# RWKV chains: four buffers for keys and products, a later second product, and another layout of the stage's tiles

## The chip, the cores and the metric

The kernel runs on one core of a Trainium2 chip. The metric is the device time of one execution in microseconds (us); less is better. A core has five engines that run side by side, each through its own list of instructions in order: TensorE (PE, matmuls, with its weight loads shown as PEld), VectorE (DVE), ScalarE (ACT), GpSimd (POOL) and SyncE (SP). SP does nothing but issue DMA transfers, one after another; 16 DMA engines carry them out. Instructions wait for each other through semaphores.

## The reference

One inference step of a backbone with four layers (retention, RWKV-7 time mixing, differential attention, neighbourhood attention), each for 128 context tokens and 512 latent tokens, 640 in all, of width 1024. The change touches the second layer, RWKV-7, whose core is this scan, for 16 heads of width 64, forwards and backwards in time:

```
def step(s, inp):
    r_t, w_t, k_t, v_t, kk_t, a_t = inp
    sa = jnp.einsum('bhvk,bhk->bhv', s, -kk_t)
    s = (s * w_t[:, :, None, :] + sa[..., None] * (kk_t * a_t)[:, :, None, :]
         + v_t[..., None] * k_t[:, :, None, :])
    return s, jnp.einsum('bhvk,bhk->bhv', s, r_t)
```

The sum of both directions is normalised by head, a bonus term is added, and the result goes through a gate and the output projection.

## The kernel before, in words

The layer has two parts. The first, `rwkv_project`, computes the projections and, pair of heads by pair of heads (eight pairs), the scaled queries and keys; `rwkv_prepare` writes them to DRAM (`wd_q`, `wd_bk`, and the pieces `wd_lt`, `wd_lb` of a triangular matrix). The second part, `rwkv_mix`, reads them back and runs the chains. Time is cut into 10 chunks of 64 tokens; within a chunk the scan becomes small matrix products, with the inverse of a triangular 64 x 64 matrix for each chunk, direction and head, and only a short chain from chunk to chunk is left. The steps of a pair p in `rwkv_mix` are:

- `rwkv_inverse` (L1300): inverts the 32 x 32 diagonal blocks by 31 steps of two vector instructions, a product into `wtmp` (L1312) and a subtraction from `wX` (L1314). It loads `wN` (L1306), stores the inverse (L1315), copies its transpose into `wN` (ACT, L1317) and stores that (L1318). For pairs 0 to 2 DVE does it during the projections; for pairs 3 to 7 it is POOL, during the chains. There `wN` has two buffers and `wX` has one.
- `inverses` (L1380): loads the inverted blocks into `wTT` (L1390) and `wLB`, `wTM` (L1385, L1386), and makes the off-diagonal blocks by two sets of 80 small matmuls (L1398). The first set's result goes into `wPZ` (L1403), the second's, from `wPZ` and `wTT`, into `wTT` (L1405 on DVE, L1407 on ACT).
- `scores` (L1408): loads the keys `wKK` (L1414), the products `wBK` (L1415) and the queries `wR` (L1417); transposes the keys (L1424) into `wQT`, multiplies keys with BK (L1431, masked into `wQT`, L1433), `wQT` with `wTT` (L1441), BK with R (L1449), scales BK and transposes it into `wBT` (L1473); loads the values `wUV` and their copy `wRS` and the start states.
- `chain` (L1494): eight steps, each a set of matmuls (L1504), a copy on ACT, a set of matmuls (L1511) and updates on DVE.
- `read` (L1527) and `finish` (L1542): the outputs into the PSUM tile `wy`, the normalisation on DVE, two multiplications on POOL (with `wgb`, L1565, and with the bonus, L1567), a transposition (L1570), the gate `wsg` (L1572) and the store (L1573).

Tiles of one name share buffers: a new one waits until the last user of the buffer is done. `wKK` and `wBK` have two buffers, and each pair takes two, one for each direction. Most others have one for even and one for odd pairs. All of them lie in SBUF in the order of the list `order2`, with those that it doesn't name (`wN`, `wX`, `wtmp`, `wyc` and small ones) after them; ahead of the list come the mask, the first `wTT`, `wTM`, `wPZ` and two `wLB`, 20.75 KB for each partition. The first part of the layer used the same stretch of SBUF from the left, in the order `wxx` (20 KB), `wN`, `wX`, `wBK`, `wQ`, `wLT` and so on, with the projection weights and the hidden state from the right. The layer after it puts the output projection's weights (`wr`, `wh`, `wl`) at the right again.

The order of instructions on each engine, SP's among them, is fixed when the kernel is built: a planner simulates the run and takes, of what it holds to be ready, the instruction with the smallest priority number. `at` (L1578) sets that number: 2000 for each pair, and an offset for each step (`phase`: the chain -3, `inverses` -2.2, `scores` and the inverse -2, `finish` -1.3, `read` -0.4).

Of the kernel before, what the change touches and what calls it, by code (L numbers as in the profile page):

```python
# [10 lines left out]
AF = mybir.ActivationFunctionType  # L11
ALU = mybir.AluOpType
# [8 lines left out]
NT = 640  # L21
# [1021 lines left out]
NCH = 10  # L1043
# [29 lines left out]
class Rwkv:  # L1073
# [260 lines left out]
    def rwkv_mix(s, dr, od):  # L1334
        nc, I, O = s.nc, s.I, s.O
        v, act, pe, gp = nc.vector, nc.scalar, nc.tensor, nc.gpsimd
        H = (slice(0, 64), slice(64, 128))
        LO, HI = H
        with s.pool('w2') as w2, s.pool('w2p', space=PSUM) as pp:
            T = lambda shape, name, bufs=1, dt=F32: w2.tile(shape, dt, name=name, tag=name, bufs=bufs)  # L1340
            P = lambda name, bufs, shape=(128, 512): pp.tile(list(shape), F32, name=name, tag=name, bufs=bufs)
            z = lambda shape, name, dt=F32: w2.tile(shape, dt, name=name)
            inverse = lambda p: p in s.inv_late and s.rwkv_inverse(T, dr, p, 2)

            u64, u128 = [128, 2, 20, 64], [128, 2 * NCH, 128]
            bt, rr, qa = [128, NCH, 128], [128, 2, NCH, 2, 64], [128, 2 * NCH, 2, 64]
# [3 lines left out]
            TTs = [z(u128, 'wTT0')]  # L1350
            TM, PZ = z([128, 2 * NCH, 32], 'wTM'), z([128, 2 * NCH, 32], 'wPZ')
            LBs = [z([128, 2 * NCH, 32], f'wLB{k}') for k in range(2)]
# [3 lines left out]
            for k in s.order2:  # L1356
                if k == 'TT1':
                    TTs.append(z(u128, 'wTT1'))
                elif k == 'fin':
                    for n, sh, b in (('vt', [128, 5, 128], 1), ('sg', [128, NT], 1), ('yc', [128, 10, 64], 1), ('gb', [128, 128], 1), ('SW', [128, 4, 64], 2),  # L1360
                                     ('st0', [128, 64], 2), ('SF', [128, 2, 64], 1), ('so', [64, 2, 64], 2)):
                        T(sh, 'w' + n, b)
                elif k == 'misc':
                    for n, sh, b in (('gb', [128, 128], s.fin_bufs['gb']), ('st0', [128, 64], s.st_bufs), ('SF', [128, 2, 64], 1), ('so', [64, 2, 64], s.st_bufs)):
                        T(sh, 'w' + n, b)
                elif k[:3] == 'pad':
                    w2.tile([128, int(k[3:])], F32, name='w' + k)
                elif k in ('vt', 'sg'):
                    T([128, 5, 128] if k == 'vt' else [128, NT], 'w' + k, s.fin_bufs[k])
                elif k[0] == 'R' and k[1] in '01':  # L1370
                    Rs[int(k[1])][int(k[2])] = query(int(k[1]), int(k[2]))
                else:
                    T({'QT': u128, 'KK': [128, NCH, 64], 'BK': [128, NCH, 128], 'RR': rr, 'QA': qa, 'BT': bt, 'RS': u64, 'UV': u64}[k[:2]], 'w' + k,
                      2 if k in ('KK', 'BK') else 1)
            for t in (*TTs, *Rs[0], *Rs[1]):
                gp.memset(t, 0.0)
            st_ = {}
# [2 lines left out]
            def inverses(p):  # L1380

                TT, LB, tt_d, tq_d = TTs[p % len(TTs)], LBs[p % 2], dr['tt'][p], dr['tq'][p]
                for h in range(2):
                    a = h * 64
                    nc.sync.dma_start(out=LB[a:a + 32], in_=dr['lb'][p][h])  # L1385
                    nc.sync.dma_start(out=TM[a:a + 32], in_=tq_d[h].rearrange("u s t -> s u t"))  # L1386
                for blk in (1, 0):
                    for h in range(2):
                        a = h * 64 + blk * 32
                        nc.sync.dma_start(out=TT[a:a + 32, :, a:a + 32], in_=tt_d[blk, h].rearrange("u s t -> s u t"))  # L1390

                for prod in range(2):
                    ps = [P('wtp', 2, (128, 16, 32)) for _ in range(2)]
                    for u in range(20):
                        for h in range(2):
                            a = slice(h * 64 + 32 * prod, h * 64 + 32 * prod + 32)
                            l, r = (LB[a, u, :], TM[a, u, :]) if prod == 0 else (PZ[a, u, :], TT[a, u, h * 64 + 32:h * 64 + 64])
                            pe.matmul(ps[h][u % 4 * 32:u % 4 * 32 + 32, u // 4, :], l, r, start=True, stop=True)  # L1398
                    for h in range(2):
                        for j in range(4):  # L1400
                            src = ps[h][j * 32:j * 32 + 32, :5, :]
                            if prod == 0:
                                (v.tensor_copy if h else act.copy)(PZ[h * 64 + 32:h * 64 + 64, j::4, :], src)  # L1403
                            elif h:
                                v.tensor_scalar(out=TT[64:96, j::4, 96:128], in0=src, scalar1=-1.0, scalar2=None, op0=ALU.mult)  # L1405
                            else:
                                act.activation(out=TT[0:32, j::4, 32:64], in_=src, func=AF.Copy, scale=-1.0)  # L1407
            def scores(p):  # L1408
                cols = slice(p * 128, p * 128 + 128)
                KK, BK, R, BT = {}, {}, Rs[p % 2], {}  # L1410
                QT, RR = T([128, 2 * NCH, 128], 'wQT'), T(rr, f'wRR{p % 2}')
                for d in range(2):
                    KK[d], BK[d] = T([128, NCH, 64], 'wKK', 2), T([128, NCH, 128], 'wBK', 2)
                    nc.sync.dma_start(out=KK[d].rearrange("p c t -> p (c t)"), in_=dr['q'][p][d, 0])  # L1414
                    nc.sync.dma_start(out=BK[d].rearrange("p c t -> p (c t)"), in_=dr['bk'][p][d])  # L1415
                    for i in range(2):
                        nc.sync.dma_start(out=R[d][H[i], :, i, :], in_=dr['q'][p][d, 1, H[i]].rearrange("p (c t) -> p c t", t=64))  # L1417

                QTp = QT.rearrange("p (q i) k -> p q (i k)", i=2)
                for q0 in range(0, NCH, 4):  # L1420
                    n = min(4, NCH - q0)
                    ps = P('wtp', 2, (128, 4, 128))
# [4 lines left out]
                for d in range(2):  # L1427
                    pa = [P('wsc', 2, (128, 8, 64)) for _ in range(2)]
                    for c in range(NCH):
                        for i in range(2):  # L1430
                            pe.matmul(pa[i][H[c % 2], c // 2, :], KK[d][H[i], c, :], BK[d][H[i], c, 64:128], start=True, stop=True)  # L1431
                    for i in range(2):
                        v.tensor_tensor(out=QTp[:, d * 5:d * 5 + 5, 64 + i * 64:128 + i * 64], in0=pa[i][:, :5],  # L1433
                                        in1=mask[:, 0:1, :].to_broadcast([128, 5, 64]), op=ALU.mult)

                TT = TTs[p % len(TTs)]
                QA = T(qa, f'wQA{p % 2}')
                for u0 in range(0, 20, 4):
                    ps = P('wsc', 2, (128, 4, 128))
# [4 lines left out]
                for d in range(2):  # L1444
                    for c0 in range(0, NCH, 4):
                        n = min(4, NCH - c0)
                        ps = P('wsc', 2, (128, 4, 128))
# [4 lines left out]
                for d in range(2):  # L1452
# [16 lines left out]
                    for c0 in range(0, NCH, 4):  # L1469
                        n = min(4, NCH - c0)  # L1470
                        ps = P('wtp', 2, (128, 4, 128))
# [4 lines left out]
                for i in range(2):  # L1476
                    for d in range(2):
                        src = dr['vr' if d else 'v'][:, cols].rearrange("(c t) (i d) -> i t c d", t=64, i=2)[i]
# [4 lines left out]
                for d in range(2):  # L1483
                    st = T([128, 64], 'wst0', s.st_bufs)
                    nc.sync.dma_start(out=st, in_=I['state_rwkv'][0, 0, d, 2 * p:2 * p + 2].rearrange("i v k -> (i v) k"))
                    ps = P('wtp', 2, (128, 8, 64))
# [91 lines left out]
            def at(part, fn, p, *args):  # L1578
                s.tc.cur_priority = first + int(s.scale * (p + s.phase[part]))
                return fn(p, *args)  # L1580

            at('inv', inverse, 0)
            at('whole', inverses, 0)
            at('score', scores, 0)
            at('inv', inverse, 1)
            at('whole', inverses, 1)
            at('score', scores, 1)
            at('inv', inverse, 2)
            for p in range(8):
                at('chain', chain, p)  # L1590
                if p < 6:
                    at('whole', inverses, p + 2)
                ps = at('read', read, p)
                if p < 6:
                    at('score', scores, p + 2)
                    if p < 5:
                        at('inv', inverse, p + 3)
                at('fin', finish, p, ps)
# [171 lines left out]
class Kernel(Net, Ret, Rwkv, Diff, Na, Run):  # L1770
    hp = (600, 1, 1, 1, 300, 0, 0)
    preps = {'r': (2, 2, 2, 2)}
    bkv = 1
    order2 = ('KK', 'BK', 'RR1', 'QT', 'QA1', 'BT00', 'UV0', 'BT10', 'RS0', 'BT01', 'BT11', 'R01', 'RS1', 'R10', 'UV1', 'R11', 'TT1', 'QA0', 'RR0', 'R00', 'misc', 'pad448', 'vt', 'sg')
    todo_ret = [(0, 4), (0, 5), (1, 0), (1, 1), (1, 2), (1, 3), (1, 4), (1, 5)]
    todo_rwkv = []
    todo_t = {0: [(2, 0), (2, 1), (2, 2), (2, 3), (2, 4), (2, 5)], 1: [(3, 0), (3, 1), (3, 2), (3, 3), (3, 4), (3, 5)]}
# [28 lines left out]
    scale = 2000  # L1806
# [37 lines left out]
```

## Time and profile before

| | |
|---|---|
| median of 3 runs | 2563.71 us (2556.4 to 2573.88) |
| the profiled execution's own time | 2563.22 us |
| its span, first to last instruction | 2561.5 us |
| PE busy | 2314.2 us (90%), 18951 matmuls |
| DVE, ACT, POOL busy | 1442.0 (56%), 1115.7 (44%), 730.3 us (29%) |
| mean granted clock of TensorE | 0.935 of full speed |
| DMA | 303.54 MB in 353575 packets, 150489 of them under 512 B |

Busy time is the time in which an engine had an instruction in work, and an engine that waits for another is not busy. The shares are means over four layers with different limits, so the stage of the change has to be read by itself.

### The profile page before, as it was taken

Reading aid. Unit: us, or ns where it says so; the run is one execution under the profiler, and the core shown is the slowest. Engines: PE = TensorE matmul, PEld = TensorE weight load, DVE = VectorE, ACT = ScalarE, POOL = GpSimd, SP = SyncE. Lnnn points to the kernel's source line nnn. Section 1 sums busy time; section 2 is a strip of 40 time slices with the busy share of each in tenths; the row PEclk is TensorE's granted clock in tenths of the full one; section 3 lists DMA queues with packets and bytes.
Section 4 is the critical chain, followed back from the end, with each engine's and each line's share of the span. In section 5 each row is a group of like instructions: output and inputs, shape, how many; then the busy total and the mean of one; then the engine's idle time right before and its main releaser. Section 6 shows DMA issues by size and latency. Waiting matters only on the chain. (4 is left out here: it accounts for less than half of the span.)

```text
span 2561.5 us, 48738 instructions
## 1 busy us (share of the span) xinstructions
PE 2314.2 (90%) x18951; PEld 2086.4 (81%) x18951; DVE 1442.0 (56%) x3369; ACT 1115.7 (44%) x2565; POOL 730.3 (29%) x694
## 2 busy tenths in 40 slices
PE   7999999997989899876988887899898898999998
PEld 4889898987959789776877777588888888898888
DVE  6534344443173888772555564667766665654454
ACT  5323333333144655544545442345555534655551
POOL 3323232413210000013666503333323233333221
PEclk9999999998999889987879988899999998999999
DMA  8432333325273467756454634511111122322221
GB/s 292 132 109 89 110 115 114 106 80 191 79 245 107 130 211 214 221 172 155 135 145 128 169 109 149 179 54 56 48 47 48 44 74 60 78 76 65 76 72 58
DMA packets 353575, 303.54 MB, mean 119 GB/s; under 512 B 150489, under 2 KB 291313, under 8 KB 353345
## 3 DMA queue, kind: packets, MB, share of 16 engines
q1 hardware_dynamic: 353344, 300.44, 39.6%
q8 instruction: 149, 2.44, 0.4%
q14 instruction: 82, 0.66, 0.1%
HBM read 231.37 MB, written 64.79 MB: 116 GB/s over the span
## 5 line engine op out<-in xcount | busy, mean ns | idle before, releaser
L93 POOL TENSOR_TENSOR wl<-wr,wh 128x1024 fp32r<-128x1024 f32 (+1 forms) x168 | 371.8, 2227 | 668.2 <-ACT wh L170 526.6
L88 PE MATMUL pj<-hH,wh 128*128 128x320 f32 x1280 | 405.8, 319 | 11.0 <-ACT hH L96 7.6
L89 PE MATMUL pj<-hL,wh 128*128 128x320 f32 x1280 | 405.2, 317 | 2.7 <-POOL hL L93 1.8
L90 PE MATMUL pj<-hH,wl 128*128 128x320 f32 x1280 | 402.3, 315 | 0.1
L88 PEld LDWEIGHTS pj<-hH,wh 128*128 128x128 f32 x1280 | 244.7, 192 | 24.6 <-ACT hH L96 10.8
L89 PEld LDWEIGHTS pj<-hL,wh 128*128 128x128 f32 x1280 | 245.0, 191 | 10.5 <-POOL hL L93 4.6
L90 PEld LDWEIGHTS pj<-hH,wl 128*128 128x128 f32 x1280 | 244.9, 191 | 2.3 <-issue 1.0
L170 ACT CAST wh<-wr 128x1024 fp32r<-128x1024 f32 x168 | 175.4, 1047 | 122.0 <-PE pj L89 52.7
L88 PE MATMUL oa<-oh,wh 128*128 128x384 f32 (+1 forms) x640 | 200.3, 314 | 18.8 <-ACT wh L170 14.7
L88 PE MATMUL pj<-wh,hH 128*128 128x256 f32 x640 | 190.4, 298 | 13.0 <-DVE dr L756 8.5
L89 PE MATMUL oa<-ol,wh 128*128 128x256 f32 (+1 forms) x640 | 198.1, 311 | 0.7 <-DVE ol L93 0.6
L90 PE MATMUL oa<-oh,wl 128*128 128x256 f32 (+1 forms) x640 | 197.7, 311 | 0.0
L89 PE MATMUL pj<-wl,hH 128*128 128x256 f32 x640 | 188.0, 294 | 0.0
L90 PE MATMUL pj<-wh,hL 128*128 128x256 f32 x640 | 187.5, 293 | 0.0
L88 PEld LDWEIGHTS pj<-wh,hH 128*128 128x128 f32 x640 | 129.8, 203 | 21.1 <-DVE dr L756 9.6
L88 PEld LDWEIGHTS oa<-oh,wh 128*128 128x128 f32 x640 | 121.8, 191 | 22.2 <-ACT wh L170 15.0
L89 PE MATMUL pj<-wxl,wh 128*128 128x320 f32 x416 | 132.9, 322 | 4.2 <-DVE wxl L93 4.2
L90 PE MATMUL pj<-wxh,wl 128*128 128x320 f32 x416 | 131.7, 320 | 1.2 <-DVE wl L93 1.2
L88 PE MATMUL pj<-wxh,wh 128*128 128x320 f32 x416 | 131.4, 324 | 1.0 <-ACT wxh L96 1.0
L89 PEld LDWEIGHTS pj<-wl,hH 128*128 128x128 f32 x640 | 129.7, 203 | 0.0
L90 PEld LDWEIGHTS pj<-wh,hL 128*128 128x128 f32 x640 | 129.6, 202 | 0.0
L89 PEld LDWEIGHTS oa<-ol,wh 128*128 128x128 f32 x640 | 122.1, 191 | 1.5 <-DVE ol L93 1.3
(480 smaller groups left out, 5633.0 us busy)
## 6 DMA issues: line engine op xcount, KB each, us to landing
wr<-in_ret_w_in SPq DMA_DIRECT2D x48, 512.0 KB
wm<-in_w_mod SPq DMA_DIRECT2D x40, 512.0 KB
wr<-in_w_mod SPq DMA_DIRECT2D x32, 512.0 KB
wr<-in_rwkv_w_in SPq DMA_DIRECT2D x32, 512.0 KB
wl<-in_w_mod SPq DMA_DIRECT2D x24, 512.0 KB
wr<-in_diff_w_in SPq DMA_DIRECT2D x48, 256.0 KB
wr<-in_na_w_in SPq DMA_DIRECT2D x48, 256.0 KB
wd_bk<-wBK SPq DMA_DIRECT2D x16, 640.0 KB
```

The lines of the kernel that those rows point to most:

```text
L88: mm(out, l[0], r[0], start=start, stop=False)
L89: mm(out, l[0], r[1], start=False, stop=False)
L90: mm(out, l[1], r[0], start=False, stop=stop)
L93: eng.tensor_tensor(out=lo, in0=src, in1=hi.bitcast(F32), op=ALU.subtract)
L170: nc.scalar.copy(hi[:, :, :n], raw[:, :, :n])
```

## The change

Five edits, all for `rwkv_mix`. `wKK` and `wBK` get four buffers each. The late inverses' `wN` gets one buffer (the default of `rwkv_inverse`) in place of two. The second set of small matmuls of the inverse, with its copies, becomes a function `product(p, 1)` that `scores` calls after the masked products and before the product of `wQT` with `wTT`; the first stays in `inverses`. The list `order2` is sorted anew: KK and BK go from its head almost to its end, the small tiles (`misc`: `wgb`, start and end states), `wvt` and `wsg` go from its end into its middle, `wyc` is named there too, and a pad of 1.75 KB goes. No instruction is added or removed.

```diff
-            inverse = lambda p: p in s.inv_late and s.rwkv_inverse(T, dr, p, 2)
+            inverse = lambda p: p in s.inv_late and s.rwkv_inverse(T, dr, p)
...
-                elif k in ('vt', 'sg'):
-                    T([128, 5, 128] if k == 'vt' else [128, NT], 'w' + k, s.fin_bufs[k])
+                elif k in ('vt', 'sg', 'yc'):
+                    T({'vt': [128, 5, 128], 'sg': [128, NT], 'yc': [128, 10, 64]}[k], 'w' + k, s.fin_bufs.get(k, 1))
...
-                      2 if k in ('KK', 'BK') else 1)
+                      4 if k in ('KK', 'BK') else 1)
...
-                for prod in range(2):
-                    ps = [P('wtp', 2, (128, 16, 32)) for _ in range(2)]
-                    for u in range(20):
...
+                product(p, 0)
+
+            def product(p, prod):
+
+                TT, LB = TTs[p % len(TTs)], LBs[p % 2]
+                ps = [P('wtp', 2, (128, 16, 32)) for _ in range(2)]
+                for u in range(20):
...
-                    KK[d], BK[d] = T([128, NCH, 64], 'wKK', 2), T([128, NCH, 128], 'wBK', 2)
+                    KK[d], BK[d] = T([128, NCH, 64], 'wKK', 4), T([128, NCH, 128], 'wBK', 4)
...
                         v.tensor_tensor(out=QTp[:, d * 5:d * 5 + 5, 64 + i * 64:128 + i * 64], in0=pa[i][:, :5],
                                         in1=mask[:, 0:1, :].to_broadcast([128, 5, 64]), op=ALU.mult)
+                product(p, 1)
...
-    order2 = ('KK', 'BK', 'RR1', 'QT', 'QA1', 'BT00', 'UV0', 'BT10', 'RS0', 'BT01', 'BT11', 'R01', 'RS1', 'R10', 'UV1', 'R11', 'TT1', 'QA0', 'RR0', 'R00', 'misc', 'pad448', 'vt', 'sg')
+    order2 = ('RR1', 'QT', 'QA1', 'BT00', 'UV0', 'BT10', 'RS0', 'misc', 'vt', 'sg', 'yc', 'BT01', 'BT11', 'R01', 'RS1', 'R10', 'UV1', 'R11', 'TT1', 'RR0', 'KK', 'BK', 'QA0', 'R00')
```

## Rows read from the trace of the kernel before

**Rows 1.** Stretches: length; busy PE, PEld, DVE, ACT, POOL; granted clock; DMA share; GB/s.
```profile
1144.00:1157.00 13.00, 0.71 (x22) 0.61 (x15) 2.63 (x11) 2.97 (x5) 2.24 (x1) 0.50 0.79 241
1157.00:1176.00 19.00, 16.95 (x188) 14.79 (x187) 5.38 (x10) 12.15 (x33) 1.26 (x1) 0.91 1.07 192
...
1192.00:1500.00 308.00, 282.48 (x4531) 240.95 (x4530) 175.46 (x498) 157.88 (x407) 186.32 (x342) 0.87 0.53 137
...
1386.00:1426.00 40.00, 35.54 (x623) 29.62 (x621) 21.38 (x60) 21.41 (x56) 28.88 (x56) 1.00 0.55 145
```

**Rows 2.** Waits of PE from 1135 to 1565: total us, times, longest.
```profile
PE wsc L1431 <- issue: 13.4, 1, 13.4
PE wy L1570 <- DVE wyc L1568: 12.5, 3, 12.0
PE wtp L1424 <- DMA wKK<-wd_q: 12.3, 1, 12.3
PE wsc L1431 <- DMA wBK<-wd_bk: 5.2, 4, 1.9
...
PE wtp L1398 <- DVE wPZ L1403: 2.3, 2, 1.7
...
PE wtp L1424 <- DVE wTT L1405: 2.1, 2, 1.2
PE wtp L1398 <- DMA wR<-wd_q: 1.8, 1, 1.8
```

**Rows 3.** Timeline of the entry: start, length, instruction, [idle before, what ended it].
```profile
1133.05 0.31 PE L90 MATMUL pj<-wxh,wl 128*128 128x320 f32 x1
...
1147.62 0.29 SPq L1318 DMA_DIRECT2D wd_tq<-wN  x1
...
1149.29 1.00 SPq L1415 DMA_DIRECT2D wBK<-wd_bk  x2
...
1156.54 1.30 PE L1424 MATMUL wtp<-ident,wKK 128*128 128x128 f32 x5 [12.29 <-DMA wKK<-wd_q]
...
1187.26 2.04 SPq L1306 DMA_DIRECT2D wN<-wd_lt  x2
1189.43 0.34 SPq L1415 DMA_DIRECT2D wBK<-wd_bk  x1
1189.82 1.08 PE L1431 MATMUL wsc<-wBK,wKK 64*64 64x64 f32 x26 [13.42 <-issue]
...
1192.96 0.23 POOL L1312 TENSOR_TENSOR wtmp<-wX,wN 80x31 f32<-80x31 f32 x1 [28.19 <-DMA wN<-wd_lt]
```

**Rows 4.** DMA from 1138 to 1192.
```profile
DMA packets 21127, 10.68 MB, mean 198 GB/s; under 512 B 18522, under 2 KB 19290, under 8 KB 21124
```

**Rows 5.** Waits of SP's queue from 1200 to 1480: total us, times, longest.
```profile
SPq L1415 <- PE wtp L1473: 31.7, 7, 12.9
```

**Rows 6.** Timeline, all engines, from one late inverse to the next.
```profile
1402.52 0.27 POOL L1314 TENSOR_TENSOR wX<-wX,wtmp 80x31 f32<-80x31 f32 x1
...
1404.83 0.29 SPq L1318 DMA_DIRECT2D wd_tq<-wN  x1
...
1406.82 0.23 POOL L1312 TENSOR_TENSOR wtmp<-wX,wN 80x31 f32<-80x31 f32 x1
...
1407.55 0.85 SPq L1386 DMA_DIRECT2D wTM<-wd_tq  x2
```

**Rows 7.** The tile wX, 1190 to 1460: min/median/max ns, first and last start.
```profile
L1314 POOL TENSOR_TENSOR wX<-wX,wtmp x155: 247/587/1125, 1193.3 to 1450.2; 80x31 f32<-80x31 f32 x10, 80x60 f32<-80x60 f32 x10, 80x87 f32<-80x87 f32 x10, 80x112 f32<-80x112 f32 x10
```

**Rows 8.** Timeline of PE: the first product of QT and TT of pair 7.
```profile
1477.69 1.62 PE L1441 MATMUL wsc<-wTT,wQT 128*128 128x128 f32 x12
```

**Rows 9.** The tile wTT, copies of the second product on DVE: min/median/max ns.
```profile
L1405 DVE TENSOR_SCALAR wTT<-wtp x32: 315/321/329, 1145.6 to 1474.0; 32x160 f32<-32x160 f32 x32
```

**Rows 10.** Timeline of ACT at the exit: casts of the output projection's weights.
```profile
1546.42 1.04 ACT L170 CAST wh<-wr 128x1024 fp32r<-128x1024 f32 x1 [5.96 <-POOL wyc L1565]
...
1549.58 1.05 ACT L170 CAST wh<-wr 128x1024 fp32r<-128x1024 f32 x1 [2.12 <-DVE wyc L1572]
```

More of the change, by code (lines that the diff above doesn't have):

```diff
@@ L1390, in inverses @@
                         nc.sync.dma_start(out=TT[a:a + 32, :, a:a + 32], in_=tt_d[blk, h].rearrange("u s t -> s u t"))
-                for prod in range(2):
-                    ps = [P('wtp', 2, (128, 16, 32)) for _ in range(2)]
-                    for u in range(20):
[L1395 to L1398, printed above, removed]
-                    for h in range(2):
[L1400 to L1407, printed above, removed]
@@ new lines, in inverses @@
+                product(p, 0)
[3 more added lines that the diff above has]
+                for u in range(20):
+                    for h in range(2):
+                        a = slice(h * 64 + 32 * prod, h * 64 + 32 * prod + 32)
+                        l, r = (LB[a, u, :], TM[a, u, :]) if prod == 0 else (PZ[a, u, :], TT[a, u, h * 64 + 32:h * 64 + 64])
+                        pe.matmul(ps[h][u % 4 * 32:u % 4 * 32 + 32, u // 4, :], l, r, start=True, stop=True)
+                for h in range(2):
+                    for j in range(4):
+                        src = ps[h][j * 32:j * 32 + 32, :5, :]
+                        if prod == 0:
+                            (v.tensor_copy if h else act.copy)(PZ[h * 64 + 32:h * 64 + 64, j::4, :], src)
+                        elif h:
+                            v.tensor_scalar(out=TT[64:96, j::4, 96:128], in0=src, scalar1=-1.0, scalar2=None, op0=ALU.mult)
+                        else:
+                            act.activation(out=TT[0:32, j::4, 32:64], in_=src, func=AF.Copy, scale=-1.0)
```

## The prediction

> **What bounds the kernel now.** I read four views in this order: busy time by stretch, to find the stage that the change touches and what limits it; the waits of TensorE (PE) in it; the timeline at the stage's two ends; the handover between two inverses. The stage, the RWKV chains, runs from about 1138 to 1553 us of a span of 2561.5. Nothing outside it and its borders is edited.
>
> In the stage's middle PE is the bound: 282 of 308 us busy at a mean granted clock of 0.87 of 2.4 GHz, while its best 40 us ran at 1.00 and held 623 matmuls [rows 1]. At that density the 4531 matmuls of the middle need 4531 x 40 / 623 = 291 us. The mix of shapes is not the same, so this is rough, but it says that some 17 us can be won there, not 60. At the stage's entry PE is not the bound: in 1144 to 1157 it is busy for 0.7 of 13 us, at the 1.2 GHz level, and the DMA engines work at 0.79 and then, in 1157 to 1176, at a share of 1.07, which is all there is [rows 1].
>
> PE's waits say the same [rows 2]: two at the entry (12.3 us for the keys KK of pair 0, and 13.4 us ahead of the scores of pair 1, put down to "issue"), one of 12.0 us at the exit (the finish of pair 7), and in between only crumbs, of which four for BK, 5.2 us together, and a few around the inverses' second product.
>
> **The change part by part.** No instruction is added or removed: the 16 loads each of KK and BK, the 80 matmuls and 8 copies of each second product and the 5 late loads of N stay. What changes is when each may start, and the order on PE and on SP's queue that the planner makes of it.
>
> *Four buffers for KK and BK, at another place.* Two buffers hold just the two directions of one pair, so the next pair's loads wait for this pair's last transposes.
> First stall: the loads of pair 0 are issued at 1149.29, behind the store of the inverse's transposed block from N at 1147.62, and PE starts at 1156.54, so issue to use is 7.2 us [rows 3]. By the tile sizes in the code KK and BK now begin at 20.75 KB of their pool; the projections' pool before has 20 KB of xx and then N, X and its own BK there, so the loads sit on bytes that the last early inverse uses until that store. After the change they sit behind some 156 KB, past most of those tiles, on bytes of the weights, whose last matmul starts at 1133.05 [rows 3]. The loads can so go out up to 16 us earlier. PE has its own work until 1144.2 (12.3 us before 1156.5) and would then need KK at once. I take 10 of the 12.3 us as won; the bounds are 0 (the queue delivers no sooner) and 12.3.
> Second stall: BK of pair 1 goes out last at 1189.43, and PE resumes at 1189.82 [rows 3]. With spare buffers both loads can stand right behind those of pair 0's scores. But the queue is full: between 1138 and 1192 the engines moved 10.68 MB in 21127 packets, 18522 of them under 512 B [rows 4]. KK and BK are rows of 2.5 and 5 KB, few of these packets, so the order in which they are asked for matters more than their size. I take 5 of 13.4 us (bounds 0 and 13.4), nearer to the full queue's row. Entry together: 15 us, between 0 and 25.7.
> Middle: the four waits for BK go, 5.2 us. SP also stood 31.7 us, 7 times and once for 12.9, at a BK load that waited for the transposes [rows 5], with everything behind it in the queue; the loads of R and the states behind it cost PE 1.8 us at most in its own rows [rows 2], so I count no more for it. I take 5 us; the bounds are 0 and the 17 us above.
>
> The Trainium skill's page "DMA: Bandwidth & Descriptors", section Specifications, puts the smallest transfer for line rate at 512 B. The trace agrees: with the share rising from 0.79 to 1.07 the rate falls from 241 to 192 GB/s. By that rule alone the entry would be bound by small packets that the change doesn't touch, and its 15 us would be 0; that is rival C.
>
> *One buffer for the late inverses' N in place of two.* Here time is lost. The inverses of pairs 3 to 7 run one after the other on GpSimd (POOL). Between two of them 4.0 us pass now, from the last subtraction's end at 1402.79 to the next product at 1406.82, since the next N lies there already [rows 6]. With one buffer its load must wait for the store from N, issued at 1404.83. The load of TM that needs this store went out at 1407.55, 2.7 us later [rows 6], and from a load of N to POOL's first product took 1187.26 to 1192.96, 5.7 us [rows 3]. So the next inverse starts at 1404.83 + 2.7 + 5.7 = 1413.2, 6.4 us later than now; four handovers make 26 us. What covers it: the last inverse ends at 1450.4 [rows 7], and the step that needs it, the product of QT and TT of pair 7, starts at 1477.7 [rows 8], 27 us later. From the end to that step some 17 us are needed as it stands (store, load, two small products with their copies), so 10 us are free. But if the pairs come 20 us earlier the cover shrinks by that, unless the first N arrives earlier as well, which it can: POOL waited 28.2 us for it [rows 3], and its buffer lies on bytes long free. I take +6 us; the bounds are 0 and 26.
>
> *The second product later.* It moves behind the transposes of KK and the small scores. Removed: the waits of the transposes for the copies into TT (2.1 us the longest row) and part of the waits for PZ (2.3) [rows 2]. Added: the product with QT now follows directly on the copies, four of 0.32 us on DVE [rows 9], as many on ACT beside them, 1.3 us a pair, 10 us over eight pairs if nothing stands between. Chain steps and reads of other pairs, which the planner puts between, hide it now and can hide it there; if they don't, it costs the 10. Taken: 0; bounds -4 and +10.
>
> *The last steps' tiles in the middle of SBUF.* After the stage the output projection's weights lie over them: the first cast waits 5.96 us for the multiplication with gb on POOL, to 1546.42, the second 2.12 us for the last step on sg, to 1549.58 [rows 10]. Meanwhile PE stands 12.0 us. With the casts free, matmuls on chunks that are loaded fill part of that hole; the last chunk still comes through the finish, a store and a load, so what lies behind it doesn't move. I take 6 us, between 0 and 12.
>
> Sum: -15 -5 +6 +0 -6 = -20 us. The profiled execution took 2563.2 us (span 2561.5 and 1.7 around it), the median of the runs is 2563.7, so no correction: **2543 us**.
>
> **Rivals.**
> A, the forecast, 2543 (2533 to 2553): the entry's stalls shrink, part of it is paid back on POOL.
> B, the middle follows too: entry -22, middle -15, exit -8, POOL hidden: -45, 2518. For it: clock 0.87 where 1.00 is reached; against: only 5.2 us of the waits are BK's.
> C, the entry is bound by the DMA engines, or the loads keep their place in SP's queue, so that the buffers do nothing: -5 at the exit, 2558. For it: the share of 1.07; against: 0.79 in the very stretch of the first stall.
> D, slower (2567 to 2610): the inverses become the bound. Place: the load of N behind the store, on SP, four times. If the first inverse starts no earlier and each handover costs 6.4 us, the last ends at 1476 and the step that needs it starts at 1493, not 1477.7: +16, and the entry's 15 us are void, since this step then sets the time. The N loads also stand in SP's queue ahead of R and the values, four times 2.7 us, of which I count half, +5; the exit gives 6 back: +15, 2578. It decides as soon as the handovers add more than the 10 us of cover and what POOL gains at the start. Against it: POOL stood idle for 28.2 us at the start, time that can be used.
>
> **Numbers.** Chances: A 0.50, B 0.20, C 0.16, D 0.14. The range goes from B's middle to D's first half: 2518 to 2572. A run of this kernel can't tell less than about 1%, 25.6 us, from no change: below 2538 lie B and a third of A, 0.36; above 2589 lies the upper half of D, 0.07; the rest, 0.57, is within.
>
> **What would show it.** Right: PE's wait for KK near 2 us and the scores of pair 1 under way before 1180; no PE wait and no SP wait on BK; the weight casts ahead of 1540; POOL's handovers near 10 us, yet the last inverse not ended later than before. Wrong: the entry's two waits unchanged in sum (C); PE waiting for PZ or TT in pairs 5 to 7 by more than 5 us (D); a mean clock above 0.93 in the middle (B).

## The result and the profile after

The changed kernel takes 2547.34 us (median of 6 runs, 2543.93 to 2549.91), the kernel before, on the same chip, 2564.74 us (2556.4 to 2573.88): a ratio of 0.9935, 95% interval 0.9915 to 0.9955. That is 17.4 us less, within 1%. The profiled execution of the change took 2549.91 us (span 2548.1), that of before 2563.2 (span 2561.5), 13.4 us apart in span.

The forecast was 2543 us. The total is 4 us off it, but it is made of other parts than the prediction's sum. Both traces are cut at four marks: the end of the last projection matmul of this layer, the first chain step, the end of the last read, the end of the last matmul of the output projection. The three stretches between the marks are called entry, middle and exit below. First before, then after (columns as in [rows 1]):

```profile
1133.40:1192.40 59.00, 27.05 (x443) 23.27 (x443) 14.69 (x38) 19.37 (x51) 6.94 (x5) 0.67 0.88 207
1192.40:1535.50 343.10, 310.80 (x4974) 264.81 (x4971) 195.21 (x558) 165.01 (x426) 189.11 (x344) 0.86 0.51 133
1535.50:1614.20 78.70, 62.93 (x420) 58.86 (x420) 40.41 (x75) 21.97 (x33) 28.22 (x15) 0.91 0.42 136
```

```profile
1150.00:1199.90 49.90, 33.08 (x483) 28.55 (x482) 18.97 (x45) 18.88 (x49) 41.24 (x67) 0.68 0.84 211
1199.90:1520.70 320.80, 300.59 (x4955) 256.45 (x4955) 194.81 (x547) 164.21 (x425) 133.24 (x222) 0.91 0.56 144
1520.70:1599.30 78.60, 61.85 (x391) 57.01 (x393) 43.28 (x81) 20.96 (x35) 18.55 (x11) 0.89 0.38 126
```

So the projections end 16.6 us later (1150.0 for 1133.4), the entry is 9.1 us shorter, the middle 22.3, the exit the same; what lies behind it is 1.6 us longer. Together -13.3.

In the middle PE does the same work, about 4960 matmuls. Busy time times granted clock, a rough measure of that work at full clock, is 310.8 x 0.86 = 267 us before and 300.6 x 0.91 = 274 after. So the work didn't shrink. What falls is PE's time at the 1.2 GHz level (a mean granted clock of 0.91 instead of 0.86), which shows as 10.2 us less busy time, and its idle time, 32.3 to 20.2 us.

PE's waits from 1135 to 1565 after the change (total us, times, longest), beside [rows 2]:

```profile
PE oa L88 <- ACT oh L96: 9.5, 3, 7.3
PE wsc L1435 <- DMA wBK<-wd_bk: 9.0, 2, 7.5
PE wz L88 <- ACT wt L1246: 7.0, 1, 7.0
...
PE wy L1575 <- DVE wyc L1573: 6.2, 4, 4.8
...
PE wtp L1428 <- DMA wKK<-wd_q: 1.3, 1, 1.3
```

Of the 12.3 us for KK 1.3 are left, the 13.4 us ahead of the scores of pair 1 are 7.5, the 12.0 us for the last finish 4.8. New are 7.0 us of the projections (wz) and 7.3 us at the output projection (oa).

The largest difference was in no row of the prediction: POOL's late inverses (columns as in [rows 7]), and the first product of pair 7, which needs the last of them:

```profile
L1314 POOL TENSOR_TENSOR wX<-wX,wtmp x155: 246/612/3953, 1075.8 to 1375.9; 80x31 f32<-80x31 f32 x10, 80x60 f32<-80x60 f32 x10, 80x87 f32<-80x87 f32 x10, 80x112 f32<-80x112 f32 x10
```
```profile
1461.83 2.47 PE L1446 MATMUL wsc<-wTT,wQT 128*128 128x128 f32 x10 [0.17 <-DVE wTT L1408]
```

They start at 1075.8 instead of 1193.3 and end 74 us earlier, although from the end of one to the first product of the next 12.6, 28.9, 13.2 and 8.4 us pass now (before: 12.4, 10.8, 4.0 and 4.0). By the tiles' addresses N and X lie above 207 KB now, past the projections' last weight buffers, which end at 204 KB; before, N and X lay on those buffers. So the first late inverse runs beside the projections. Before and after, from 1128 to 1138:

```profile
1128.00:1138.00 10.00, 7.29 (x91) 6.50 (x89) 9.74 (x21) 3.31 (x9) 1.97 (x5) 0.93 0.70 202
```
```profile
1128.00:1138.00 10.00, 5.05 (x49) 4.65 (x48) 5.20 (x7) 0.87 (x3) 9.14 (x15) 0.94 0.09 33
```

Beside POOL's 9.14 us, DVE is busy for 5.20 us instead of 9.74, ACT for 0.87 instead of 3.31, and the DMA engines' share falls from 0.70 to 0.09. Two queues stand at POOL, by after's timeline of ACT and PE and by the waits of SP's queue from 1130 to 1500:

```profile
1137.26 1.95 ACT L1317 COPY wN<-wX 40x1024 f32<-40x1024 f32 x1 [9.13 <-POOL wX L1314]
...
1140.49 0.64 PE L88 MATMUL wz<-wta,wB 128*128 128x320 f32 x1 [7.04 <-ACT wt L1246]
```
```profile
SPq L1421 <- PE wy L1544: 21.7, 6, 6.8
SPq L1419 <- PE wtp L1478: 16.1, 6, 5.1
...
SPq L1421 <- POOL wX L1314: 8.8, 1, 8.8
```

ACT waits 9.13 us to copy the inverse into N, with the projections' activations behind that copy. SP waits 8.8 us at a load of R, L1421, into a tile that POOL has to clear first, with the projections' stores behind it.

### The profile page after: what moved, and what is told of

The parts are those of the page before. It is cut to its first block, busy times and chain, and to the rows that moved or that the text cites. A ratio compares the mean times of both kernels' runs of the same rounds, so it can differ in the third digit from the quotient of the medians.

```text
span 2548.1 us, 48737 instructions
## 1 busy us (share of the span) xinstructions
PE 2318.3 (91%) x18951; PEld 2087.3 (82%) x18951; DVE 1462.0 (57%) x3369; ACT 1115.0 (44%) x2565; POOL 756.6 (30%) x694
## 5 line engine op out<-in xcount | busy, mean ns | idle before, releaser
L88 PE MATMUL oa<-oh,wh 128*128 128x384 f32 (+1 forms) x640 | 200.9, 317 | 27.6 <-ACT wh L170 14.9
L89 PE MATMUL oa<-ol,wh 128*128 128x384 f32 (+1 forms) x640 | 200.1, 314 | 1.2 <-DVE ol L93 1.1
```

The source lines that it names most:

```text
L88: mm(out, l[0], r[0], start=start, stop=False)
L89: mm(out, l[0], r[1], start=False, stop=False)
```

## The experiments

order_only and bk4_only are the kernel before with one part of the change, late_X_nb2 has two edits; all others are the changed kernel with one. Times are medians; ratios are to the kernel before, run on the same chip in turn. Cuts of code are shortened. A table of marks, read from each kernel's profiled execution (us): where the projections end, and the length of entry, middle and exit as above.

```
                  time    ratio (95%)              proj. ends  entry  middle  exit
before            2563.2  (profiled execution)     1133.4      59.0   343.1   78.7
after             2547.3  0.9935 (0.9915-0.9955)   1150.0      49.9   320.8   78.6
nb2               2559.0  0.9987 (0.9970-1.0004)   1150.5      58.7   320.0   79.2
bk2               2573.4  1.0034 (1.0018-1.0051)   1148.4      53.2   352.2   76.7
kk2               2562.7  1.0008 (0.9991-1.0025)   1150.6      50.9   336.6   80.1
prod_early        2545.6  0.9929 (0.9909-0.9950)   1148.3      48.9   319.3   79.4
tail_end          2562.4  0.9998 (0.9979-1.0016)   1148.3      50.7   323.0   93.8
late_N            2581.2  1.0081 (1.0054-1.0107)   1132.1      49.5   373.6   78.6
late_X            2540.8  0.9913 (0.9889-0.9937)   1131.0      48.2   335.9   76.7
late_X_nb2        2544.1  0.9925 (0.9901-0.9950)   1133.2      50.6   338.0   76.7
copy_pool         2551.3  0.9949 (0.9930-0.9967)   1138.1      62.9   318.7   79.8
short_inv         2543.3  0.9917 (0.9892-0.9941)   1140.1      51.3   325.3   78.5
order_only        2556.0  0.9977 (0.9958-0.9996)   1134.3      49.7   344.2   79.3
bk4_only          2557.6  0.9987 (0.9970-1.0003)   1150.0      54.4   328.2   81.4
```

**The buffers of KK and BK (bk2, kk2).**

```diff
-  4 if k in ('KK', 'BK') else 1      # and in scores: wKK 4, wBK 4
+  2 if k in ('KK', 'BK') else 1      # bk2: wKK 2, wBK 2; order2: ..., 'BK', 'pad3840', 'QA0', ...
+  {'KK': 2, 'BK': 4}.get(k, 1)       # kk2: wKK 2, wBK 4; order2: ..., 'KK', 'pad1280', 'BK', ...
```

> The changed kernel with two buffers for KK and BK, and a pad in place of the other two, so that every other tile keeps its address. Theory 1 (the gain of the middle is POOL's head start): loses 4 us at most, 2545 to 2552, POOL's inverses where they are, the steady time per pair near 41.5 us. Theory 2 (the gain is the buffers': SP is no longer blocked, so loads, then the scores of the next pair, come earlier): loses most of the 17 us, 2557 to 2566, with SP waiting for the transposes again 12 us at a time and 44 us per pair.

> The changed kernel with two buffers for KK and four for BK, a pad in the room of the other two KK, so that every other tile keeps its address. KK is free after the small scores of its pair, BK only after the transposes at the end of its scores. If it is BK that holds the queue (SP at the BK load, all else behind it): 2545 to 2552, nothing lost. If KK's loads, which stand ahead of BK's and R's in the queue, block as much: 2560 to 2575. Half the loss, 2553 to 2560, would say that both count.

bk2 lost 26 us, more than either theory of it gave, and the middle alone 31.4 us (352.2 for 320.8), with POOL's inverses as early as in the changed kernel (1074.4 to 1386.9). So POOL's head start alone doesn't shorten the middle; it takes the buffers. (That they do it without a head start isn't shown: see late_X and late_N below.) The middle of bk2, then of kk2, and bk2's waits of SP's queue and of PE from 1200 to 1500:

```profile
1201.60:1553.80 352.20, 321.22 (x4998) 272.95 (x4995) 192.13 (x551) 165.00 (x423) 131.99 (x222) 0.85 0.51 130
```
```profile
1201.50:1538.10 336.60, 305.77 (x4955) 259.61 (x4955) 193.79 (x547) 166.28 (x425) 132.68 (x222) 0.89 0.54 137
```
```profile
SPq L1419 <- PE wtp L1478: 37.0, 11, 6.9
SPq L1421 <- PE wy L1544: 31.8, 10, 9.7
```
```profile
PE wsc L1435 <- DMA wBK<-wd_bk: 5.3, 4, 3.5
```

SP stands 37.0 us at BK's loads (16.1 after) and 31.8 at R's (21.7). Of the 31.4 us, 10.8 are PE's idle time (31.0 for 20.2), with 5.3 us of waits for BK; the other 20.6 are busy time for the same work (321.2 us for 300.6), at a clock of 0.85 for 0.91.

With four BK but two KK half of the 31.4 comes back; 15.8 us stay lost, and the time, 2562.7, lies where I had put it if KK's loads block as much as BK's. But 9.8 of the 15.8 us are one wait of PE. kk2's ACT and PE:

```profile
1264.29 1.95 ACT L1317 COPY wN<-wX 40x1024 f32<-40x1024 f32 x1 [9.27 <-POOL wX L1314]
...
1266.79 1.44 PE L1446 MATMUL wsc<-wTT,wQT 128*128 128x128 f32 x5 [9.80 <-ACT wQA L1447]
```

ACT stood at the copy of POOL's inverse into N, and the copies into QA that PE needed stood behind it. In the changed kernel no PE wait of the middle is longer than 1.3 us. So this is the order on ACT that came with two KK, and what the buffers of KK are worth apart from it, some 6 us by this difference, isn't shown.

**The second product (prod_early).**

```diff
                 product(p, 0)
+                product(p, 1)         # and no product(p, 1) behind the small scores
```

> The changed kernel with the second product of the inverses right behind the first, as before. If its place matters (theory 3): slower by 4 to 15 us, PE waiting for PZ and TT in the rows of the middle. If not (the prediction's zero; theories 1 and 2): 2543 to 2551.

2545.6 us with nearly the interval of the changed kernel: its place makes no difference that can be measured, and theory 3 (the place matters) falls.

**The last steps' tiles (tail_end).**

```diff
-  order2 = (..., 'RS0', 'misc', 'vt', 'sg', 'yc', 'BT01', ..., 'QA0', 'R00')
+  order2 = (..., 'RS0', 'BT01', ..., 'QA0', 'R00', 'misc', 'vt', 'sg', 'yc')
```

> The changed kernel with the tiles of each pair's last steps (gb, st0, SF, so, vt, sg, yc) at the end of the order instead of the middle; the tiles behind them move down by their size, N and X stay. By the prediction: 6 us slower (0 to 12), the first casts of the output weights waiting for the finish of pair 7, the first output matmuls at 1540 or later instead of 1496. By what the trace of the change shows (the exit takes 80 us from the last read to layer 3 with or without it): 0 to 2 us, since the last chunk through the finish, a store and a load sets the end there.

15 us slower, more than either case of the expectation, and nearly all in the exit (93.8 for 78.6). Its PE, SP and ACT there:

```profile
1542.46 0.88 PE L1575 MATMUL wy<-ident,wyc 128*128 128x128 f32 x3 [20.44 <-DVE wyc L1573]
```
```profile
1544.65 0.32 SPq L1578 DMA_DIRECT2D wd_o<-wyc  x1
1545.06 0.99 SPq L160 DMA_DIRECT2D wr<-in_rwkv_w_out  x2
```
```profile
1550.42 1.04 ACT L170 CAST wh<-wr 128x1024 fp32r<-128x1024 f32 x1 [14.81 <-DMA wr<-in_rwkv_w_out]
```

PE stands 20.4 us with no matmul of the output projection to put there, since the last two loads of its weights go out only behind the store that ends the last finish, and the cast waits 14.8 us for them. With 15 KB more for KK and BK the tiles at the end lie 13 to 15 KB higher than in the kernel before, whose loads had come by then and whose casts waited for 6.0 and 2.1 us [rows 10]. The middle of SBUF is thus worth 15 us to this kernel, and nothing against the kernel before, whose exit was 78.7: it cures a cost that the buffers bring.

**One buffer for N (nb2).**

```diff
-  s.rwkv_inverse(T, dr, p)
+  s.rwkv_inverse(T, dr, p, 2)
```

> The changed kernel (2547 us) with two buffers for the late inverses' N again, everything else kept. Theory 1 (the middle gains because POOL's late inverses start some 117 us earlier, from the place of N and X at the far end of SBUF, and not because of their number): POOL's first late inverse still starts near 1076, the handovers shrink from 14 to 29 us to below 10 us, the time is 2542 to 2549, as the handover is hidden. Theory 2 (the handover of a single N costs what the prediction put there, 6 us): 2541 or less, with the last inverse 20 us or more earlier and the middle shorter. If the single buffer had helped, it would be above 2552.

Neither of the two theories: 12 us slower, most of it in the entry (58.7 for 49.9), the middle unchanged (320.0). Waits of SP's queue (1120 to 1170) and of PE (1085 to 1175):

```profile
SPq L1315 <- POOL wX L1314: 15.2, 1, 15.2
SPq L1421 <- POOL wtmp L1312: 11.5, 1, 11.5
```
```profile
PE wn L1282 <- ACT wLT L1283: 11.7, 1, 11.7
```

With the second N the store of the first late inverse, L1315, came to stand earlier in SP's order, and SP stood there 15.2 us, until 1136.7. That isn't the loss, as the changed kernel's SP stands until 1137.0, at a load of R. The loss is the next stand, 11.5 us. nb2's POOL and SP, then the changed kernel's SP:

```profile
1147.53 7.29 POOL L1312 TENSOR_TENSOR wtmp<-wX,wN 80x135 f32<-80x135 f32 x1
...
1155.29 1.16 POOL L1376 MEMSET wR<- 128x1280 f32 x1
1156.48 1.20 SPq L1421 DMA_DIRECT2D wR<-wd_q  x2
1157.77 1.08 SPq L1288 DMA_DIRECT2D wd_lt<-wLT  x2
```
```profile
1148.30 1.06 SPq L1288 DMA_DIRECT2D wd_lt<-wLT  x2
```

POOL's second inverse starts at 1142.4 instead of 1149.8, as its N is there already, and a zeroing of R now stands behind several of its steps, one of which took 7.29 us. SP waits for that at R's load, and the stores of LT behind it go out 9.5 us later; ACT's next copy into LT, and so PE, waits for them. The single N helped by the order that it led to, not by itself.

**One part alone on the kernel before (order_only, bk4_only).** order_only is the new order2 with everything else as before; bk4_only four KK and BK and one N at the old order without its pad.

> The kernel before (2563 us) with the new order of the tiles alone: two buffers for KK, BK and N, the second product at its old place. If the layout alone gives the entry's gain (KK and BK on bytes free early, wait for KK 12.3 us gone): 2545 to 2556. If the two buffers make the early loads void or the layout only shifts waits (theory: the gain is the buffers' alone): 2558 to 2572. If the layout harms by itself, as the run with two buffers for KK and BK of 2573 us suggests: above 2568.

> The kernel before with four buffers for KK and BK and one for N alone (the room for them), the old order of tiles (the last steps' tiles stay at the end, KK and BK at the head), the second product at its old place. Theory 2 (the middle's gain is the buffers'): the stretch from the first chain to the last read falls from 343 to 320 to 328 us, wherever the tiles lie; KK's wait of 12 us at the entry stays, since they still lie on bytes held until 1147; the exit is dearer by some 11 us, as in the run with the last tiles at the end: 2555 to 2565 in all. Rival (buffers and layout are needed together): the middle stays above 335 us, 2565 or more.

The new order alone gives the entry's gain, 9.3 us, and nothing in the middle (344.2 for 343.1): 0.9977. Four buffers alone give 14.9 us in the middle, 4.6 in the entry, and lose 16.6 at the projections, as their 15 KB push N and X beyond 204 KB and POOL starts at 1076 here too, and 2.7 in the exit: 0.9987.

**POOL's start (late_N, late_X, late_X_nb2).** late_N puts N at the head of the order, on bytes that the last early inverse holds; late_X puts X on bytes of the projections' last weights and leaves N at the far end; late_X_nb2 has two N besides.

```diff
+                elif k == 'N':                               # late_N; late_X has 'X' and 'wX'
+                    T([80, 32, 32], 'wN')
-  order2 = ('RR1', ..., 'BK', 'QA0', 'R00')
+  order2 = ('N', 'RR1', ..., 'BK', 'QA0', 'R00')       # late_N
+  order2 = ('RR1', ..., 'BK', 'X', 'QA0', 'R00')       # late_X
```

> The changed kernel (2547 us) with the late inverses' N at the head of the stage's tiles, on bytes that the projections and the last early inverse hold until about 1145, so that POOL can't start its first late inverse among the projections; all other tiles move up by the 4 KB, X stays. Theory E (POOL's inverse beside the projections is what ends them 13 to 17 us later than before, through DVE's slower instructions and ACT's queue): the last layer-2 projection matmul ends near 1135, the middle stays at 320 us, the time is 2530 to 2538. Rival 1 (POOL's head start is needed, a late start makes the inverses the bound of the middle): projections near 1135, PE waiting for PZ and TT by more than 10 us, 2545 to 2560. Rival 2 (the projections end late for another reason, such as the order on SP): projections still end near 1150, 2543 to 2552.

> The changed kernel (2547 us) with the late inverses' X, which POOL fills first, moved from the far end to between BK and QA0, on bytes of the projections' weights that are held until their last matmul; N stays at the far end, so its load goes out early as before, and only POOL's start is held back, to about 1135 to 1160 instead of 1076. Theory E (POOL's first late inverse beside the projections costs them 15 to 17 us; four buffers need POOL early, but not that early): projections end near 1134, the middle stays at 318 to 326 us since the last inverse ends some 40 to 60 us later than 1376 and is needed only near 1445, the time is 2528 to 2538. Rival 1 (60 us later is too late, with one N the inverses bound the middle): middle above 335 us, 2545 to 2565. Rival 2 (X's place or the order on SP spoils the entry as in the run with two N, where SP stood 15.2 us at an inverse's store): chain 0 starts no earlier than 1195, 2543 to 2550.

> The kernel with the late inverses' X on the bytes of the last weights, and two buffers for N. If, with POOL's later start, the handover counts (a single N's load behind the store): 2 to 8 us less than that kernel with one N, 2524 to 2534. If SP is blocked at an inverse's store in the entry again, as it was with two N at the far end (15.2 us): 8 to 14 us more than with one N, chain 0 starting later by that. If neither: within 3 us of it.

In all three the projections end at 1131 to 1133, 17 to 19 us earlier: POOL's inverse beside them is what delays them. For late_N I had expected 2530 to 2538, or 2545 to 2560 if a late start binds the middle; it took 2581.2. There POOL starts at 1205 and ends at 1477.5, as N's load stands late in SP's order; the waits of POOL (1130 to 1500) and of PE (1190 to 1560):

```profile
POOL wtmp L1312 <- DMA wN<-wd_lt: 61.8, 5, 43.1
```
```profile
PE wch L1511 <- DVE wRS L1524: 13.7, 33, 1.4
PE wch L1518 <- ACT wUV L1512: 13.5, 16, 5.8
PE wtp L1403 <- DMA wTM<-wd_tq: 7.3, 4, 3.0
```

The inverses bound the middle, 373.6 us: the chains run alone, PE waits at each of their steps, and the first product of QT and TT of pair 7 starts at 1499.9. That is rival D of the prediction, made by one edit.

late_X starts POOL at 1132.7, and chain 0 20.8 us earlier than the changed kernel; but its middle gives 15.1 us back:

```profile
1179.10:1515.00 335.90, 308.06 (x4955) 262.30 (x4955) 193.23 (x547) 166.53 (x426) 167.74 (x291) 0.88 0.55 141
```

I had expected 2528 to 2538 and got 2540.8, the lowest time of all kernels. It beats the kernel before; against the changed kernel (0.9913 beside 0.9935) the intervals overlap, so a gain there isn't shown. Late inverses aren't the reason of its longer middle: late_X_nb2 has the last one 28 us earlier (1404.7 for 1433.1) and a middle of 338.0. This stays open. With POOL's later start the second N wins nothing that shows either: 2544.1 for 2540.8, where I had expected 2 to 8 us less if the handover counted.

**What POOL's head start does to the projections (copy_pool, short_inv).**

```diff
-  nc.scalar.copy(Q_, X_[0:40]...)
+  (gp.tensor_copy if p in s.inv_pool else nc.scalar.copy)(Q_, X_[0:40]...)    # copy_pool
-  for j in range(31):
+  for j in range(1 if p in s.inv_pool else 31):                               # short_inv
```

> The changed kernel (2547 us) with the late inverses' transposed copy into N on POOL, behind the last subtraction, instead of ACT. In the changed kernel ACT stands 9.13 us at that copy (1137.26, released by POOL's X) with the projections' activations behind it, and PE then 7.0 us. If this queue on ACT is part of what ends the projections 17 us later: the last projection matmul at 1140 to 1144 instead of 1150, 2538 to 2543. If it is all POOL's load beside DVE: still 1148 to 1151, 2545 to 2550, and 1 to 2 us more per handover on POOL, which is hidden.

> The changed kernel with only the first of the 31 steps in POOL's five late inverses: their results are left wrong, all loads, stores and copies stay. It prices POOL's steps as a whole. Theory E (POOL's steps beside the projections cost them 15 to 17 us): the projections end at 1132 to 1136. Middle: if only the order that four buffers allow counts, the stretch from the first chain to the last read stays at 316 to 324 us and the time is 2528 to 2534; if POOL's steps beside the chains slow DVE and so PE, it falls to 300 to 312 us, 2512 to 2524. If the projections still end near 1150, theory E falls.

copy_pool: without the copy in ACT's queue the last projection matmul ends at 1138.1, 12 us earlier, where I had expected 6 to 10, yet chain 0 starts at 1201.0 and nothing is won: 2551.3 for the 2538 to 2543 expected in that case. The wait has moved to SP; its queue (1115 to 1160), DVE (1136 to 1156), PE (1150 to 1205, the wait that began before 1138):

```profile
SPq L1421 <- POOL wR L1376: 13.4, 2, 12.9
```
```profile
DVE wBK L1267 <- DMA wd_bk<-wBK: 9.4, 1, 9.4
```
```profile
PE wn L1282 <- DVE wQ L1271: 12.0, 1, 12.0
```

SP stands 12.9 us at the load of R, since the zeros of that tile (L1376) stand in POOL's queue behind the inverse; the store of the projections' BK stands behind the load, DVE waits for the store, PE for DVE. short_inv: without POOL's steps the projections end at 1140.1 and the last product of their preparation at 1147.9 (1154.5 after, 1137.6 before), so about 7 to 10 of the 17 us are the steps' own length, where I had expected 15 to 17. The rest stays with the inverses' loads, stores and copies early in the queues, which I take for its cause; no run removes them alone. Its middle, 325.3 us, is not shorter than the changed kernel's: POOL's steps beside the chains cost the middle nothing that shows.

## Why the prediction held in its total and not in its parts

That the total came within 4 us is luck. By the profiles the sum lacks a cost of 16.6 us at the projections, and its term for the middle is 17.3 us too small; the two cancel. Of the smaller misses, the entry won 5.9 us less than its term, the exit 5.9 less, and POOL cost 6 less.

*Entry, -15.* Right as far as it went. KK's 12.3 us became 1.3, pair 1's 13.4 became 7.5 (I had taken 10 and 5 as won), and the stretch is 9.1 us shorter, not 15. order_only, whose projections end as early as before, gives 9.3 with two buffers, and KK's wait is gone there: this is the place's doing. Its wait for pair 1's BK is nearly as long as before, so a share of the spare buffers in the entry doesn't show (PE's waits, 1130 to 1195):

```profile
PE wsc L1431 <- DMA wBK<-wd_bk: 11.7, 2, 11.1
```

Rival C falls: the DMA share of the entry is still 0.84, and the stretch shrank all the same.

*What the sum left out, +16.6.* The prediction saw that N's first load could come early and booked it as relief: "POOL stood idle for 28.2 us at the start, time that can be used". The step that failed is that an earlier start was taken to cost nothing. It put a 61 us inverse (1075.8 to 1137.2) beside the projections, ahead of things that two other queues need from POOL: N's copy on ACT and R's load on SP, which waits for POOL's zeros. late_X, late_N and order_only, where POOL starts at 1133 to 1205, all end the projections at 1131 to 1134.

*Middle, -5, measured -22.3.* The mis-sized term. The step was that "the loads of R and the states behind it cost PE 1.8 us at most in its own rows, so I count no more for it". bk2 shows 31.4 us for the buffers, and bk4_only, on the kernel before, 14.9. PE's rows show a small part of it (5.3 us for BK in bk2): two thirds of the 31.4 are busy time at a lower clock, so a term read from waits had to come out too small. My reading, which no run isolates, is that a late load moves the next pair's scores and leaves PE with chain steps alone for a while. The prediction's second estimate, that 17 us were to be won if the middle ran at its best density, was nearer, and so was rival B's middle, 15; B's sign, a clock above 0.93 in the middle, was not reached (0.91). Nor was the sign of no SP wait on BK: SP still stands 16.1 us there.

*POOL, +6, measured 0.* The prediction read 4.0 us off the last handover and took it for all four; before, they were 12.4, 10.8, 4.0 and 4.0. They grew from 31 to 63 us together, 32 us where 26 was the forecast, and not by N's load alone: the first one before and the longest one after are mostly waits for the store of X, which has one buffer in both kernels. POOL before, then POOL and SP after:

```profile
1238.67 0.95 POOL L1307 MEMSET wX<- 80x1024 f32 x1 [8.72 <-DMA wd_tt<-wX]
```
```profile
1221.81 0.95 POOL L1307 MEMSET wX<- 80x1024 f32 x1 [24.50 <-DMA wd_tt<-wX]
```
```profile
1214.29 0.39 SPq L1315 DMA_DIRECT2D wd_tt<-wX  x1
```

That inverse had ended at 1197.3; SP issued loads of the next pairs before its store. All this is hidden by the head start: the last inverse ends at 1376.2, 86 us before pair 7's product. late_N shows the bill without it, a middle of 373.6 us.

*Second product, 0.* Right (prod_early).

*Exit, -6, measured 0.* The cover was there: the first matmul of the output projection runs at 1495.97 instead of 1553, and PE's wait is 4.8 us instead of 12.0. It was lost on the way through the last finish, 20.4 us from read to end for 14.0 before, as splits of the output projection's inputs (`ol`) stand between its steps on DVE, and a split of its weights on POOL holds one of these steps up for 2.2 us. That the weights came free is not the whole reason: tail_end, where no cast of a weight falls into the last finish, takes 22.6 us for it. After's DVE, POOL and ACT:

```profile
1529.78 1.28 DVE L93 TENSOR_TENSOR ol<-oraw,oh 128x128 fp32r<-128x128 f32 x2
1530.97 2.36 DVE L124 TENSOR_SCALAR wrsy<-wvar 128x10 int32<-128x10 int32 x1
1533.36 0.17 DVE L125 TENSOR_SCALAR wrsy<-wrsy 128x10 int32<-128x10 int32 x1
```
```profile
1530.91 2.38 POOL L93 TENSOR_TENSOR wl<-wr,wh 128x1024 fp32r<-128x1024 f32 x1 [13.60 <-ACT wh L170]
```
```profile
1546.14 1.26 ACT L96 CAST oh<-oraw 128x128 fp32r<-128x128 f32 x2 [15.31 <-DMA oraw<-wd_o]
```

The last chunk still comes through finish, store and load (1546.14, for which PE waits 7.3 us), so what ran early was not on the path.

Open: why late_X's middle is 15 us longer than the changed kernel's, and why bk2's is 9 us longer than that of before, which has two buffers too. Clearing R on another engine, or ahead of the inverse, which copy_pool's rows suggest, was not tried.

## What to carry to other kernels

Where a tile lies decides when its first user may start, and an engine that starts earlier takes its in-order queue along: ask not only what the early work frees, but what else stands behind it on that engine and on the queues that wait for its results. Where PE is the bound and its clock moves, a blocked load queue shows only in part as a wait of PE (bk2: 10.8 us idle of 31.4); read PE's busy time, clock and idle time for the same number of matmuls as well. Look for the longest single wait before putting a difference down to the part that was taken out: kk2's was most of it and came from another queue. Take the parts of a change out one by one from the changed kernel as well as trying them alone: here four KK and BK are worth 26 us inside it and nothing that can be measured alone (0.9987, to 1.0003), and a part that wins nothing against before (the last tiles) is what keeps another from costing 15.

## What the runs showed of the hardware

DVE and POOL hold up each other's instructions. The 128x10 instruction of 1530.97 above took 2.36 us beside a POOL subtraction of 2.38 that had begun 0.06 us earlier; the next of its kind took 0.17. The same product of the projections (L1272, 128x640), before and then after, beside the late inverse:

```profile
L1272 DVE TENSOR_TENSOR wQ<-wr__10676,wE x2: 820/820/821, 1080.6 to 1094.9; 128x640 f32<-128x640 f32 x2
```
```profile
L1272 DVE TENSOR_TENSOR wQ<-wr__10676,wE x2: 1080/1212/1344, 1082.7 to 1103.0; 128x640 f32<-128x640 f32 x2
```

The Trainium skill's page "SBUF — State Buffer", section "SBUF: two separate sides", says that GpSimd and some kinds of VectorE's instructions take a shared pair of ports as an exclusive lock, held for a whole instruction. The trace agrees: DVE's 2.36 us ends with POOL's instruction (1533.33 and 1533.29). And it goes both ways: POOL's longest subtraction of the late inverses grew from 1.125 us [rows 7] to 3.953 beside the projections. The product of 7.29 us in nb2 above ran beside 14 instructions of DVE that followed each other with hardly a gap (DVE busy for 7.26 of the 7.29 us). The same shape in the changed kernel, in the middle:

```profile
1229.36 0.41 POOL L1312 TENSOR_TENSOR wtmp<-wX,wN 80x135 f32<-80x135 f32 x1
```
